# The third depthwise convolution moved from VectorE to ScalarE and GpSimd

## The chip, the cores and the metric

The kernel runs on one core of a Trainium2 chip. The time is the device time of one execution in microseconds; the median of several executions counts. The engines are TensorE (PE in the rows; PEld is its weight load), VectorE (DVE), ScalarE (ACT), GpSimd (POOL) and SyncE (SP).

## The reference

The program is two transformer-like blocks over 512 tokens of 1024 channels in float32. The first block's mixing stage is where the change lies. It projects the normalised input by `w_in` and splits the result. One half is a gated causal depthwise convolution of width 31 over 512 channels, with a layer norm over the channels and a silu:

```
u, u_gate = jnp.split(p_conv, 2, axis=-1)
u = u * jax.nn.sigmoid(u_gate)
u = causal_dwconv(u, conv_dw_w, conv_dw_b)          # 31 taps, 512 channels
u = jax.nn.silu(layer_norm(u, LN_EPS) * conv_ln_g + conv_ln_b)
```

The other half is an RWKV recurrence over 8 heads of 64 (`wkv7_scan`), with its own norm and gate, of which only the cost matters here. Both halves are joined and multiplied by `w_out`. A gated feed-forward follows, and then the second block (attention, feed-forward, HGRN2, feed-forward), which the change does not touch.

## The kernel before, in words

Channels lie on the 128 partitions and the 512 tokens along the free dimension, so the 512 channels of the convolution are four tiles of 128 x 512, here called the first to the fourth convolution (`i` = 0 to 3). Every dense product is made three times with float32 operands split into a high and a low part (lines 193 to 195): weights arrive by a transfer of SyncE's queue, ScalarE makes the high part `wh` (line 168) and VectorE the low part `wl` (line 169).

`conv_in(i)` (line 486) makes the convolution's input `u`: two dense products, a tanh by ScalarE into a tile `s` of the buffer "gate" (line 490), and a product by VectorE (line 491). `conv(i)` (line 493) starts its sum `acc` with a ScalarE operation that takes the first tap and the bias (line 499). The other 30 taps are VectorE operations of line 501, each of which reads the shifted `u` and `acc` and writes `acc`. The trace calls `acc` "h", since it lies in that tensor. `u` has two buffers.

The RWKV half goes by four pairs of heads. For a pair p, `wkv_prep` makes the decays and scores (VectorE masks NM and LM, lines 663 and 664). `wkv_inverse` (line 686) inverts triangular blocks. It begins on GpSimd: a transfer of NM to Ld in DRAM (line 696) and back as small blocks Gb (line 698), 15 products and 15 sums of up to 64 elements on 64 partitions (lines 705 and 707), a transposing copy into Tt (line 709), two transfers to Dd (line 714) and two back as Dm and Dt (line 715). All of these transfers are issued by GpSimd. Then TensorE and ScalarE grow the inverse (lines 717 to 762) in small products, each with a copy out of PSUM by ScalarE (lines 724, 746, 752, 756). `wkv_tail` (line 765) finishes the pair; it takes a tile from each of the single buffers "tl" (`sq`, line 807) and "gate" (`r`, line 812).

`mix_out` (line 889) multiplies by `w_out` in two parts: the first three of eight k-tiles are those of the first three pairs, the other five wait for the convolution's result and the last pair. Between them `conv_tail` (line 539) normalises the four convolutions: mean (line 546), difference (549), squares (551), variance (552), a reciprocal root (566 to 569), silu (558) and the split for the product (252, 253).

The order in each engine's queue is fixed when the program is built. The library that orders it takes an operation when its inputs are ready in a plan of its own and prefers the one that stands earlier in the program; a tile's buffer is given out in the same way. A block under `with filler(k)` (line 143) adds a million to that place, so it goes behind everything else. The third convolution is such a filler (lines 529 and 530), between `wkv_inverse` and `wkv_tail` of the third pair; so are the first part of `w_out` and `conv_tail`. The fourth convolution (line 534) is not.

Of the kernel before, what the change touches and what calls it, by code (L numbers as in the profile page):

```python
# [9 lines left out]
F32 = mybir.dt.float32  # L10
# [4 lines left out]
AF = mybir.ActivationFunctionType  # L15
# [4 lines left out]
P = 128  # L20
D = 1024
KD = 8
T1 = 512
# [53 lines left out]
MULT, ADD, SUB = ALU.mult, ALU.add, ALU.subtract  # L77
# [344 lines left out]
def mix(k):  # L422
    tc, nc, A, vec = k.tc, k.nc, k.A, k.vec
    with ExitStack() as ctx:
        banks(k, ctx, "m", a=3, b=3)
        p1 = ctx.enter_context(tc.tile_pool(name="mx1", bufs=1))
        p2 = ctx.enter_context(tc.tile_pool(name="mx2", bufs=4))
# [65 lines left out]
        def conv(i):  # L493
            acc = S.acc_u[:, i]
            for t in range(CK):
                src = us[i][:, t:t + T1]
                w = S.cw[:, 4 * t + i:4 * t + i + 1]
                if t == 0:
                    nc.scalar.activation(acc, src, AF.Identity, bias=vec("conv_dw_b", i), scale=w)  # L499
                else:  # L500
                    nc.vector.scalar_tensor_tensor(acc, src, w, acc, MULT, ADD)  # L501

# [13 lines left out]
        conv_in(0)  # L516
        gates()
        conv(0)
        wkv_inverse(k, Q[0])
        wkv_tail(k, Q[0])  # L520
        Q[2] = pair(2)
        wkv_inverse(k, Q[1])
        conv_in(1)
        wkv_tail(k, Q[1])
        conv(1)
        Q[3] = pair(3)
        conv_in(2)
        wkv_inverse(k, Q[2])
        with filler(k):
            conv(2)  # L530
# [1049 lines left out]
```

## Time and profile before

| | |
|---|---|
| median of 3 runs (lowest, highest) | 2308.98 us (2307.26, 2311.26) |
| the profiled execution | 2304.93 us |
| its span, first to last instruction | 2303.2 us |
| mean granted TensorE clock, share of full | 0.986 |
| busy share of PE, DVE, ACT, POOL | 97%, 62%, 43%, 4% |
| taps of line 501 on VectorE, all four convolutions | 120 operations, 90.3 us |

The busy shares are means over stages with different limits. The mixing stage with its product by `w_out` is the first 420 us or so of the span. In the rows below, a time at the front of a line is microseconds from the span's start; the second number is how long the operation or the group took; in square brackets stands how long the engine was idle before it and what ended the wait.

### The profile page before, as it was taken

Reading aid. Unit: us, or ns where it says so; the run is one execution under the profiler, and the core shown is the slowest. Engines: PE = TensorE matmul, PEld = TensorE weight load, DVE = VectorE, ACT = ScalarE, POOL = GpSimd, SP = SyncE. Lnnn points to the kernel's source line nnn. Section 1 sums busy time; section 2 is a strip of 40 time slices with the busy share of each in tenths; the row PEclk is TensorE's granted clock in tenths of the full one; section 3 lists DMA queues with packets and bytes.
Section 4 is the critical chain, followed back from the end, with each engine's and each line's share of the span. In section 5 each row is a group of like instructions: output and inputs, shape, how many; then the busy total and the mean of one; then the engine's idle time right before and its main releaser. Section 6 shows DMA issues by size and latency. Waiting matters only on the chain.

```text
span 2303.2 us, 38001 instructions
## 1 busy us (share of the span) xinstructions
PE 2235.7 (97%) x15280; PEld 1990.0 (86%) x15280; DVE 1429.5 (62%) x3022; ACT 979.4 (43%) x1928; POOL 100.7 (4%) x200
## 2 busy tenths in 40 slices
PE   6999798899999999999999999999999999999999
PEld 4677676688888989888899999999999999999888
DVE  6876777875652566666676666335666667666522
ACT  3535344544442465666553444224333335444321
POOL 1150330000000000000000000000000000000000
PEclk8999999899999999999999999999999999999999
DMA  9443221253233532221032222234111113222332
GB/s 318 152 128 122 76 56 55 88 170 101 92 99 95 148 104 81 67 65 53 33 122 92 86 89 92 83 94 117 56 59 62 45 47 114 92 92 92 91 118 76
DMA packets 73936, 220.11 MB, mean 96 GB/s; under 512 B 8976, under 2 KB 17616, under 8 KB 73760
## 3 DMA queue, kind: packets, MB, share of 16 engines
q1 hardware_dynamic: 68064, 206.17, 28.2%
q0 software_dynamic: 2784, 7.82, 1.5%
q10 hardware_dynamic: 2912, 3.69, 0.5%
q8 instruction: 121, 1.98, 0.4%
q14 instruction: 55, 0.45, 0.1%
HBM read 211.24 MB, written 6.85 MB: 95 GB/s over the span
## 4 chain that ended last, share of the span: by engine, by line
PE 88%; DVE 6%; ACT 3%; DMA 1%; issue 1%; SPq 0%; ACTq 0%; DVEq 0%
PE mm L194 24%; PE mm L193 24%; PE mm L195 23%; PE sb L1402 3%; DVE wl L169 1%; PE sc L1217 1%; PE sb L1192 1%; PE sa L660 1%; ACT wh L168 1%; PE sc L1235 1%; PE sa L865 1%; PE sa L1122 1%; DMA ada<-ada_wT 1%; DMA Dm<-Dd 0%; PE sb L745 0%
## 5 line engine op out<-in xcount | busy, mean ns | idle before, releaser
L193 PE MATMUL mm<-xh,wh 128*128 128x264 f32 (+4 forms) x2852 | 904.8, 317 | 11.0 <-ACT xh L252 5.7
L194 PE MATMUL mm<-xh,wl 128*128 128x264 f32 (+4 forms) x2852 | 895.8, 314 | 4.8 <-DVE wl L169 4.5
L195 PE MATMUL mm<-xl,wh 128*128 128x264 f32 (+4 forms) x2852 | 892.5, 313 | 0.1
L193 PEld LDWEIGHTS mm<-xh,wh 128*128 128x128 f32 x2852 | 536.2, 188 | 46.6 <-ACT xh L252 6.7
L194 PEld LDWEIGHTS mm<-xh,wl 128*128 128x128 f32 x2852 | 536.4, 188 | 39.3 <-DVE wl L169 8.4
L169 DVE TENSOR_TENSOR wl<-ws,wh 128x1024 fp32r<-128x1024 f32 (+3 forms) x358 | 399.9, 1117 | 273.6 <-ACT wh L168 272.8
L195 PEld LDWEIGHTS mm<-xl,wh 128*128 128x128 f32 x2852 | 536.9, 188 | 30.5 <-issue 2.1
L168 ACT CAST wh<-ws 128x1024 fp32r<-128x1024 f32 (+3 forms) x358 | 344.8, 963 | 479.1 <-PE mm L195 410.2
L194 PE MATMUL mm<-gh,wl 128*128 128x264 f32 (+2 forms) x792 | 253.3, 320 | 1.3 <-DVE wl L169 0.9
L193 PE MATMUL mm<-gh,wh 128*128 128x264 f32 (+2 forms) x792 | 252.9, 319 | 0.0
L195 PE MATMUL mm<-gl,wh 128*128 128x264 f32 (+2 forms) x792 | 252.7, 319 | 0.0
L194 PEld LDWEIGHTS mm<-gh,wl 128*128 128x128 f32 x792 | 149.6, 189 | 13.2 <-DVE wl L169 2.8
L193 PEld LDWEIGHTS mm<-gh,wh 128*128 128x128 f32 x792 | 149.5, 189 | 10.5
L195 PEld LDWEIGHTS mm<-gl,wh 128*128 128x128 f32 x792 | 149.6, 189 | 10.2
L975 DVE SCALAR_TENSOR_TENSOR fz<-mm,V,fz 128x511 f32<-128x511 f32 x88 | 65.9, 749 | 63.2 <-ACT fz L973 61.7
L501 DVE SCALAR_TENSOR_TENSOR h<-u,cw,h 128x512 f32<-128x512 f32 x120 | 90.3, 752 | 1.8 <-ACT h L499 0.5
L1402 PE MATMUL sb<-q,kt 128*128 128x64 f32 (+3 forms) x592 | 75.7, 272 | 2.2 <-DVE kt L1434 2.2
L1402 PEld LDWEIGHTS sb<-q,kt 128*128 128x128 f32 x592 | 73.5, 195 | 2.8 <-DVE kt L1434 1.0
L194 PE MATMUL mm<-oh,wl 128*128 128x264 f32 x256 | 74.9, 292 | 0.6 <-DVE wl L169 0.6
L193 PE MATMUL mm<-oh,wh 128*128 128x264 f32 x256 | 74.8, 292 | 0.1
L195 PE MATMUL mm<-ol,wh 128*128 128x264 f32 x256 | 74.4, 291 | 0.0
L973 ACT ACTIVATE fz<-mm,V 128x512 f32<-128x512 f32 x44 | 34.2, 777 | 59.9 <-PE mm L195 59.9
(512 smaller groups left out, 2828.6 us busy)
## 6 DMA issues: line engine op xcount, KB each, us to landing
ws<-w_up_t SPq DMA_DIRECT2D x44, 512.0 KB, 3.5
ws<-gate_t SPq DMA_DIRECT2D x44, 512.0 KB, 3.5
ws<-up_t SPq DMA_DIRECT2D x44, 512.0 KB, 3.5
ws<-down_t SPq DMA_DIRECT2D x34, 512.0 KB, 3.5
wa<-ada_wT SPq DMA_DIRECT2D x32, 512.0 KB, 3.7
ws<-fox_in_t SPq DMA_DIRECT2D x32, 512.0 KB, 3.5
ws<-hg_in_t SPq DMA_DIRECT2D x32, 512.0 KB, 3.5
ws<-w_in_t SPq DMA_DIRECT2D x22, 512.0 KB, 3.8
```

The lines of the kernel that those rows point to most:

```text
L168: nc.scalar.copy(hi[:, :n], st[:, :n])
L169: nc.vector.tensor_sub(lo[:, :n], st[:, :n], hi[:, :n])
L193: mm(o, hi[:, w], xh[i][:, a:b], start=start and i == 0, stop=False)
L194: mm(o, lo[:, w], xh[i][:, a:b], start=False, stop=False)
L195: mm(o, hi[:, w], xl[i][:, a:b], start=False, stop=stop and i == n - 1)
L501: nc.vector.scalar_tensor_tensor(acc, src, w, acc, MULT, ADD)
L660: nc.tensor.matmul(sc[hh][:, kind], lt[r, cs], ar[r, c], start=True, stop=True)
L865: nc.tensor.matmul(sq.ps[:, :n], k.mean, t, start=i == 0, stop=i == KD - 1)
L973: nc.scalar.activation(z, ps, AF.Identity, bias=vec("ffn_dw_b", nt), scale=wt(2))
L975: nc.vector.scalar_tensor_tensor(z[:, t:], ps[:, 0:T1 - t], wt(2 - t), z[:, t:], MULT, ADD)
L1122: nc.tensor.matmul(s, k.blk, sq[:, hs(j)], start=True, stop=True)
L1402: nc.tensor.matmul(o, kt[:, a:a + P], qv, start=True, stop=True)
```

## The change

For the third convolution (`i == 2`) a tap after the first is no longer one operation of VectorE. ScalarE multiplies the shifted input by the tap's weight into a new tile `m`, and GpSimd adds `m` to `acc`. `m` takes the existing single buffers "gate" and "tl" by turns. The first tap, the other three convolutions and the place in the program stay as they are.

```diff
                 if t == 0:
                     nc.scalar.activation(acc, src, AF.Identity, bias=vec("conv_dw_b", i), scale=w)
+                elif i == 2:
+
+                    m = p2.tile([P, T1], F32, name="cvm", tag=("gate", "tl")[t % 2], bufs=1)
+                    nc.scalar.activation(m, src, AF.Copy, scale=w)
+                    nc.gpsimd.tensor_tensor(acc, acc, m, op=ADD)
                 else:
                     nc.vector.scalar_tensor_tensor(acc, src, w, acc, MULT, ADD)
```

## Rows read from the trace of the kernel before

**Rows 1.** The page: busy time and instructions of each engine; GpSimd's busy tenths.

```profile
PE 2235.7 (97%) x15280; PEld 1990.0 (86%) x15280; DVE 1429.5 (62%) x3022; ACT 979.4 (43%) x1928; POOL 100.7 (4%) x200
...
POOL 1150330000000000000000000000000000000000
```

**Rows 2.** Busy time by stretch: start:end, length, busy us of each engine (instructions).

```profile
290.00:301.50 11.50, 11.50 (x94) 8.60 (x95) 9.71 (x21) 4.58 (x16) 0.00 (x0) 1.00 0.06 17
301.50:333.50 32.00, 30.15 (x241) 21.70 (x235) 25.64 (x42) 11.91 (x32) 17.85 (x37) 1.00 0.27 65
333.50:378.50 45.00, 44.99 (x334) 33.05 (x334) 35.56 (x59) 20.25 (x44) 0.10 (x1) 1.00 0.19 58
378.50:395.00 16.50, 8.75 (x23) 4.80 (x22) 10.41 (x17) 11.59 (x18) 0.00 (x0) 0.90 0.18 52
```

**Rows 3.** The timeline of TensorE around its two gaps.

```profile
331.26 0.39 PE L195 MATMUL mm<-xl,wh 128*128 128x512 f32 x1
333.51 1.16 PE L723 MATMUL sb<-Dm,NM 128*128 128x128 f32 x8 [1.86 <-DMA Dm<-Dd]
...
378.47 0.39 PE L195 MATMUL mm<-xl,wh 128*128 128x512 f32 x1
...
390.58 0.79 PE L193 MATMUL mm<-xh,wh 128*128 128x512 f32 x1 [5.68 <-ACT xh L252]
```

**Rows 4.** The timeline of VectorE: first and last taps of the third and fourth convolution.

```profile
293.78 1.53 DVE L501 SCALAR_TENSOR_TENSOR h<-u,cw,h 128x512 f32<-128x512 f32 x2
...
332.72 0.75 DVE L501 SCALAR_TENSOR_TENSOR h<-u,cw,h 128x512 f32<-128x512 f32 x1
...
339.66 1.54 DVE L501 SCALAR_TENSOR_TENSOR h<-u,cw,h 128x512 f32<-128x512 f32 x2 [0.47 <-ACT h L499]
...
374.74 0.75 DVE L501 SCALAR_TENSOR_TENSOR h<-u,cw,h 128x512 f32<-128x512 f32 x1
```

**Rows 5.** Line 501 by itself: duration in ns as least/median/most, first and last start.

```profile
L501 DVE SCALAR_TENSOR_TENSOR h<-u,cw,h x120: 721/747/1100, 114.5 to 374.7; 128x512 f32<-128x512 f32 x120
```

**Rows 6.** The timeline of GpSimd: the fourth pair's inverse.

```profile
301.54 0.94 POOL L696 DMA_DIRECT2D Ld<-NM  x1 [24.29 <-DVE NM L663]
307.04 0.84 POOL L698 DMA_DIRECT2D Gb<-Ld  x1 [4.56 <-DMA Ld<-NM]
310.14 0.21 POOL L705 TENSOR_TENSOR tm<-Gb,Tb 64x15 f32<-64x15 f32 x1 [2.26 <-DMA Gb<-Ld]
...
316.22 0.31 POOL L707 TENSOR_TENSOR Tb<-Tb,tm 64x64 f32<-64x64 f32 x1
...
324.48 0.62 POOL L709 COPY Tt<-Tb 64x256 f32<-64x256 f32 x1
...
328.59 0.91 POOL L715 DMA_DIRECT2D Dm<-Dd  x1 [1.84 <-ACT sq L813]
329.49 0.89 POOL L715 DMA_DIRECT2D Dt<-Dd  x1
```

**Rows 7.** Line 606 by itself, a ScalarE operation with a scale, SBUF to SBUF.

```profile
L606 ACT ACTIVATE sq<-kx,V x4: 709/712/716, 65.6 to 253.8; 128x512 f32<-128x512 f32 x4
```

**Rows 8.** The timeline of all engines: a GpSimd copy and a tap beside it.

```profile
249.73 0.60 POOL L709 COPY Tt<-Tb 64x256 f32<-64x256 f32 x1
249.89 1.00 DVE L501 SCALAR_TENSOR_TENSOR h<-u,cw,h 128x512 f32<-128x512 f32 x1
```

**Rows 9.** The timeline of all engines: VectorE beside small GpSimd operations, first and last.

```profile
245.19 0.79 DVE L816 SCALAR_TENSOR_TENSOR y<-y,lg,r 128x512 f32<-128x512 f32 x1
...
246.18 0.61 POOL L707 TENSOR_TENSOR Tb<-Tb,tm 64x48 f32<-64x48 f32 x1
...
248.53 0.78 DVE L501 SCALAR_TENSOR_TENSOR h<-u,cw,h 128x512 f32<-128x512 f32 x1
```

**Rows 10.** The timeline of ScalarE: a weight cast and the fourth gate's tanh.

```profile
322.24 0.51 ACT L168 CAST wh<-ws 128x384 fp32r<-128x384 f32 x1 [7.55 <-PE mm L195]
...
336.61 0.60 ACT L490 ACTIVATE gate<-mm 128x512 f32<-128x512 f32 x1
```

## The prediction

> **What bounds the kernel now.** I read the page first: the span is 2303.2 us, TensorE is busy in 97% of it, and GpSimd only in the first seven of the 40 slices, which is the mixing stage [rows 1]. Then the busy time of each engine in four stretches around the third convolution [rows 2]. From 290 to 378.5 us TensorE has almost no gap (86.64 of 88.5 us), VectorE is busy for 70.9 us, ScalarE for 36.7 and GpSimd for 18. From 378.5 to 395 TensorE is busy for only 8.75 of 16.5 us. So two places could give time back or lose it: the gap of 1.86 us before the matmul at 333.51, which waits for the transfer into Dm, and the long hole from 378.9 to 390.6, in which TensorE waits for the convolutions' normalisation (its mean and variance products are the only work in it) [rows 3].
>
> Where the convolutions stand in VectorE's queue decides the second. The third convolution (the one that changes) runs its 30 taps from 293.78 to 333.5 us, while TensorE has other work. The fourth runs from 339.66 to 375.5, at 45 us almost the whole of the third stretch, and its last tap is at once followed by the normalisation that TensorE then waits for [rows 4]. So the third convolution is off the path as it stands; the fourth one's end is on it. Any time that the edit costs VectorE after 339.66 moves the hole, and so the end, by as much.
>
> **Part one, what leaves VectorE.** 30 operations of 0.747 us (the median of line 501, [rows 5]) are 22.4 us, all before 333.5. TensorE idles for 1.86 us there, so this can return 1.9 us at most, and only by way of GpSimd, whose inverse of the fourth pair ends in the transfer that the gap waits for. That chain (from the Ld transfer at 301.54 to the Dm transfer at 328.59, [rows 6]) holds 30 small products and sums from 310.14 to 324.48: 14.3 us. With their undisturbed durations of 0.21 to 0.31 us and 0.08 between two, they would take about 10.3 us; the 4 us more are spent beside VectorE's operations. I take half of it as the taps' part: 2 us earlier.
>
> **Part two, ScalarE.** 30 products, each like the Square with a scale of 128x512 from SBUF to SBUF of line 606, 0.712 us [rows 7]: 21.4 us. ScalarE has 51.8 us free from 290 to 378.5 [rows 2], so as a load they cost nothing. As a wait they can cost: a small copy out of PSUM that stands behind a product is late by up to 0.71 us, and the product itself waits for its buffer (only two: "gate" and "tl", which `wkv_tail` and `conv_in` use too). I count 0 here and leave the rest to a rival.
>
> **Part three, GpSimd.** No addition of 128x512 is in the trace. Nearest are those of 64 partitions: 15 elements in 0.21 us, 64 in 0.31 [rows 6]. That is 2.04 ns an element, so 512 make 0.31 + 448 x 2.04 ns = 1.22 us, 1.30 from start to start with the 0.08 gap. From below the bound is the copy of 256 elements, 0.60 [rows 8]; from above, four times the copy (twice the elements, two inputs instead of one), 2.4. I take 1.30: 30 of them are 39 us in a chain, since each adds to the same tile.
> They can begin at 291.3 (the bias tap of line 499, then a product). Until the Ld transfer at 301.54 GpSimd does nothing: 8 additions. Its waits for transfers (302.48 to 307.04, 307.88 to 310.14, 326.75 to 328.59) take 3, 1 and 1 more. 17 are left after the Dt transfer is issued at 330.4, so they run from there to 352.5 alone, or to about 365 if each waits for an operation of VectorE (0.75). Placed in those waits, an addition is in the way of the next link at up to four points (Ld, Gb, first product, Dm) for half its 1.30 on average, 2.6 us in all. Against the 2 us of part one that leaves the Dm transfer, and with it the fourth convolution's start, 0.6 later; from 2 earlier (of which the gap holds 1.9) to 5.2 later.
>
> **Part four, what GpSimd takes from VectorE.** At 249.73 GpSimd copies 256 elements; the tap that VectorE starts at 249.89 takes 1.00 us instead of 0.747: 0.25 us lost [rows 8]. With the small operations nothing is lost: the five operations of VectorE from 245.19 to 248.53 start 0.668 apart beside GpSimd's sums of 39 to 48 elements, which themselves stretch to 0.6 [rows 9]. So the two engines exclude each other, and a long operation of GpSimd holds VectorE's. An addition reads 2 x 512 elements, four times the copy's 256: 4 x 0.25 = 1.0 us for each addition that meets a VectorE operation of two SBUF inputs (the taps, the weight splits of line 169). Bounds: 0, as for the small sums, and 1.30, the whole addition. I take 1.0, which the slope (512 x 2.04 ns) gives as well.
> The Trainium skill, SBUF — State Buffer, section "SBUF: two separate sides", says that VectorE and GpSimd share one pair of ports as an exclusive lock, held for the whole instruction, and that the other blocks fully. By the whole of 1.30 us the sum below would be 5 us larger; rows 9 speak against the whole instruction, since the small sums hold VectorE for next to nothing.
> The 13 additions before 330.4 fall where VectorE has just lost 22.4 us of work; they cost nothing. The 17 later ones fall on the fourth convolution: 17 x 1.0 = 17 us of holding, in a stretch of 45 us in which VectorE has 9.4 us to spare [rows 2]. If all of that absorbs, 7.6 us are lost; if none, 17. These gaps are waits for other engines in the order of the queue, so I let two thirds (6.3) absorb: 10.7 us.
>
> **The sum.** 0.6 + 10.7 = 11.3 us, all through the end of the fourth convolution. The profiled execution took 2304.93 us (span 2303.2 and 1.7 around it), so 2316.2 in its terms; the median of the runs lies 4.05 us above that execution, so 2320.
>
> **The rivals.**
> *A, queues block (slower still).* The orders of the queues are fixed beforehand. If additions beside VectorE run slower than the order allows for (1.30 alone, 2.0 with a tap between), the product for the next addition but one stands at the head of ScalarE's queue until its buffer is free, and behind it stand the PSUM copies of the fourth inverse, which TensorE uses at once. For: TensorE has no gap from 333.5 to 378.5 that could absorb it. Against: ScalarE is idle for more than half. 17 x 0.7 = 12 us of waiting beside the 10.7; partly the same time, so about 20 us: 2329. The buffers add to it: `wkv_tail` holds "tl" and "gate" again from 367.7, so a third convolution not done by then ends after 376.
> *B, hidden.* VectorE holds GpSimd rather than the other way round, or most of the additions come before 330. Then only the 0.6 remain: about 2309, no change. For: rows 9, where GpSimd gave way at no cost. Against: row 249.89, and 39 us of additions do not fit before 330.4.
> *C, faster.* The product behind the fourth convolution's gate is done by 322.2 (the weight cast that its buffer releases starts at 322.24), yet its tanh runs at 336.61 [rows 10], behind other ScalarE work and after "gate" came free. The second product ends at 331.65 [rows 3]. If the new order, with VectorE free and "gate" given out otherwise, puts that tanh before 331, the fourth convolution starts 6 us earlier and the normalisation with it. It wins from the point where the additions hold VectorE for less than those 6 us after 333 plus the spare: with half the holding (8.5, of which 6.3 is absorbed) it is -6.2 + 2.2 = -4 and the gap's 1.9: 2303. Against: "gate" is wanted by 15 products more.
> The Trainium skill, GPSIMD Engine Reference, section "4.1 Engine selection", advises VectorE for elementwise additions and calls GpSimd about twice as slow with two inputs; my 1.22 against 0.747 us is a ratio of 1.6, and a ratio of 2 would make the 17 additions 5 us longer. No run here shows it yet.
>
> **Chances.** Forecast 0.45 (2314 to 2328), A 0.20 (2325 to 2345), B 0.20 (2305 to 2313), C 0.15 (2298 to 2304). A measurement of this kernel can tell about 0.2% (4.6 us) from no change, so slower is 0.65, the same 0.20, faster 0.15. Likeliest: 2320. The range leaves out most of C and the upper end of A: 2305 to 2336.
>
> **What would show it.** Right: the fourth convolution's taps spread past 380, single taps of 1.3 to 2 us after 333, additions of 1.2 to 2 us on GpSimd until 350 to 365, and the hole before TensorE's matmul of 390.58 about 11 us later, with nothing after it changed. Part three is wrong if the additions take under 1 us or over 2.4 alone; part four if the taps keep 0.75 beside them. The whole is wrong if the third convolution's additions are done before 335, or if the fourth convolution starts before 334.

## The result, and the profile after

The changed kernel takes 2327.48 us (median of 4 runs, 2325.29 to 2332.21) against 2309.49 us before (4 runs, 2307.26 to 2311.26): a ratio of 1.0087, with a 95% interval of 1.0064 to 1.011. That is 18.0 us slower. The profiled execution took 2325.29 us against 2304.93, so 20.4 us more in the traces (spans 2323.5 and 2303.2).

All of it arises in the mixing stage. The hole before the matmul of line 193 ends at 411.58 us instead of 390.58 [rows 3], 21.0 later; from there to the end the two traces need 1911.9 and 1912.6 us. The busy time by stretch, which answers to [rows 2], with the columns as there:

```profile
290.00:301.50 11.50, 10.07 (x89) 7.30 (x87) 4.74 (x13) 10.05 (x26) 8.82 (x7) 1.00 0.06 18
301.50:333.50 32.00, 25.61 (x207) 19.50 (x207) 3.88 (x11) 18.29 (x39) 29.85 (x50) 0.87 0.11 28
333.50:378.50 45.00, 40.42 (x298) 28.80 (x299) 25.59 (x41) 20.90 (x43) 13.74 (x12) 0.91 0.20 52
378.50:395.00 16.50, 13.53 (x51) 8.68 (x48) 15.58 (x25) 7.84 (x13) 0.10 (x1) 0.95 0.17 45
```

VectorE, relieved of 30 taps, has almost nothing to do from 301.5 to 333.5 us (3.88 us busy, before 25.64). GpSimd is full in its place (29.85), and TensorE, which had gaps of 1.9 us in the second stretch and none in the third, now has 6.4 and 4.6 us of them. The new operations themselves, one line each (ns as least/median/most), and the two waits between them in this stage:

```profile
L504 POOL TENSOR_TENSOR h<-h,cvm x30: 1252/1272/1700, 291.8 to 346.1; 128x512 f32<-128x512 f32 x30
L503 ACT ACTIVATE cvm<-u,cw x30: 708/722/727, 291.0 to 344.7; 128x512 f32<-128x512 f32 x30
...
ACT cvm L503 <- POOL h L504: 20.6, 17, 3.4
POOL h L504 <- ACT cvm L503: 15.5, 2, 15.1
```

Of the last two lines the second is harmless: GpSimd had been idle before its first addition anyway. The first is not. 17 products stand at the head of ScalarE's queue until an addition frees their buffer, 20.6 us in all.

GpSimd's timeline, which answers to [rows 6], shows where the additions went (a line with x3 is three in a row):

```profile
291.82 8.02 POOL L504 TENSOR_TENSOR h<-h,cvm 128x512 f32<-128x512 f32 x6 [15.07 <-ACT cvm L503]
300.30 3.99 POOL L504 TENSOR_TENSOR h<-h,cvm 128x512 f32<-128x512 f32 x3 [0.46 <-ACT cvm L503]
304.23 0.95 POOL L701 DMA_DIRECT2D Ld<-NM  x1
...
309.99 4.00 POOL L504 TENSOR_TENSOR h<-h,cvm 128x512 f32<-128x512 f32 x3
313.94 0.21 POOL L710 TENSOR_TENSOR tm<-Gb,Tb 64x15 f32<-64x15 f32 x1
...
315.72 1.26 POOL L504 TENSOR_TENSOR h<-h,cvm 128x512 f32<-128x512 f32 x1
316.95 0.26 POOL L710 TENSOR_TENSOR tm<-Gb,Tb 64x48 f32<-64x48 f32 x1
...
333.09 1.26 POOL L504 TENSOR_TENSOR h<-h,cvm 128x512 f32<-128x512 f32 x1
334.30 0.95 POOL L714 COPY Tt<-Tb 64x256 f32<-64x256 f32 x1
...
336.89 3.41 POOL L504 TENSOR_TENSOR h<-h,cvm 128x512 f32<-128x512 f32 x2
340.25 0.92 POOL L720 DMA_DIRECT2D Dm<-Dd  x1
...
342.07 5.50 POOL L504 TENSOR_TENSOR h<-h,cvm 128x512 f32<-128x512 f32 x4
```

Nine additions precede the Ld transfer, three and three stand in the waits for Ld and Gb, and then nine stand between the small operations of the inverse, which are links of one chain: each behind a sum, eight of them ahead of the next product and one ahead of the copy. Two more wait ahead of the Dm transfer and four come after it. The Ld transfer is 2.7 us later than before, the first small product 3.8, the copy into Tt 9.8, the Dm transfer 11.7.

ScalarE's timeline, around what answers to [rows 10]:

```profile
332.70 0.72 ACT L503 ACTIVATE cvm<-u,cw 128x512 f32<-128x512 f32 x1 [1.00 <-POOL h L504]
333.33 0.49 ACT L168 CAST wh<-ws 128x384 fp32r<-128x384 f32 x1
...
344.71 0.72 ACT L503 ACTIVATE cvm<-u,cw 128x512 f32<-128x512 f32 x1 [0.62 <-POOL h L504]
...
346.06 0.63 ACT L812 ACTIVATE sq<-y 128x512 f32<-128x512 f32 x1 [0.23 <-POOL h L504]
...
350.20 0.69 ACT L817 ACTIVATE r<-sa,mat 128x512 f32<-128x512 f32 x1
...
355.61 0.60 ACT L490 ACTIVATE gate<-mm 128x512 f32<-128x512 f32 x1
```

The weight cast that ran at 322.24 [rows 10] now runs at 333.33, behind products that wait. VectorE's timeline shows who waits for it, and the fourth convolution, which answers to [rows 4]:

```profile
333.86 0.92 DVE L169 TENSOR_TENSOR wl<-ws,wh 128x384 fp32r<-128x384 f32 x1 [7.78 <-ACT wh L168]
334.69 0.67 DVE L806 TENSOR_TENSOR y<-y,sa 128x512 f32<-128x512 f32 x1
335.65 1.80 DVE L253 TENSOR_TENSOR xl<-h,xh 128x512 fp32r<-128x512 f32 x1 [0.28 <-ACT xh L252]
...
359.35 4.69 DVE L506 SCALAR_TENSOR_TENSOR h<-u,cw,h 128x512 f32<-128x512 f32 x6 [0.96 <-ACT h L499]
...
395.16 0.75 DVE L506 SCALAR_TENSOR_TENSOR h<-u,cw,h 128x512 f32<-128x512 f32 x1
```

Behind that split stands `y`, a step of the third pair's tail; after it the tail's square `sq`, which follows the last products. The same steps in the kernel before, `y` on VectorE, the square and the root `r` on ScalarE:

```profile
321.56 0.69 DVE L801 TENSOR_TENSOR y<-y,sa 128x512 f32<-128x512 f32 x1
...
324.99 0.63 ACT L807 ACTIVATE sq<-y 128x512 f32<-128x512 f32 x1 [0.96 <-DVE y L805]
...
326.93 0.69 ACT L812 ACTIVATE r<-sa,mat 128x512 f32<-128x512 f32 x1
```

So `y` is 13.1 us later and the square 21.1. In the kernel before `y` stood ahead of its split (326.84) in VectorE's queue, so the edit changed the order of the queue as well as the waits. The fourth convolution starts 19.7 us later than at 339.66 [rows 4], and then its taps run at their usual 0.75 us: the last addition ended at 347.6.

So the 19.0 us by which the fourth gate's tanh is late (355.61 against 336.61) have two parts. TensorE's first matmul with Dm comes at 345.09, 11.6 us later than in [rows 3]; that is GpSimd's queue. Before, the tail's root `r` was done (326.93) while that transfer was awaited, and the tanh followed the matmul by 3.1 us. Now the square and the root come after the matmul, and the tanh follows it by 10.5: 7.4 us more, which is ScalarE's queue. About 1 us of these is TensorE's: between the square and the root it runs the product of line 815 in 2.08 us instead of 1.12 (line 810 before), at a granted clock of 0.50 from 346 to 348, after it had waited for Dm. Both traces need about the same from the fourth convolution's first tap to the end of the hole (50.9 and 52.2 us).

### The profile page after: what moved, and what is told of

Its sections match the earlier page's. It is cut to its first block, busy times and chain, and to the rows that moved or that the text cites. A ratio compares the mean times of both kernels' runs of the same rounds, so it can differ in the third digit from the quotient of the medians.

```text
span 2323.5 us, 38051 instructions
## 1 busy us (share of the span) xinstructions
PE 2243.0 (97%) x15280; PEld 1994.7 (86%) x15280; DVE 1409.7 (61%) x2992; ACT 1000.3 (43%) x1958; POOL 137.1 (6%) x230
## 4 chain that ended last, share of the span: by engine, by line
PE 86%; DVE 6%; ACT 3%; POOL 2%; issue 1%; DMA 1%; SPq 0%; ACTq 0%; DVEq 0%; POOLq 0%
PE mm L194 23%; PE mm L193 23%; PE mm L195 23%; PE sb L1407 3%; POOL h L504 1%; DVE wl L169 1%; PE sc L1222 1%; PE sb L1197 1%; PE sc L1240 1%; ACT wh L168 1%; PE sa L665 1%; PE sa L1127 1%; PE sa L870 1%; DVE h L506 1%; DMA ada<-ada_wT 1%
## 5 line engine op out<-in xcount | busy, mean ns | idle before, releaser
L194 PEld LDWEIGHTS mm<-xh,wl 128*128 128x128 f32 x2852 | 537.9, 189 | 41.9 <-DVE wl L169 10.3
L506 DVE SCALAR_TENSOR_TENSOR h<-u,cw,h 128x512 f32<-128x512 f32 x90 | 67.2, 747 | 1.6 <-ACT h L499 1.0
```

The source lines that it names most:

```text
L194: mm(o, lo[:, w], xh[i][:, a:b], start=False, stop=False)
```

## The experiments

Theory 1 is GpSimd's queue: the additions between the links of the inverse make the Dm transfer late. Theory 2 is ScalarE's queue with the two buffers: a product waits at its head, and the tail and the fourth gate behind it. The prediction's own theory is that the additions hold VectorE's taps. Diffs are against the changed kernel unless the kernel before is named; the ratios are to the kernel before, run on the same chip.

**Additions without products** (the weights of the 30 taps are left out).

```diff
-                    m = p2.tile([P, T1], F32, name="cvm", tag=("gate", "tl")[t % 2], bufs=1)
-                    nc.scalar.activation(m, src, AF.Copy, scale=w)
-                    nc.gpsimd.tensor_tensor(acc, acc, m, op=ADD)
+                    nc.gpsimd.tensor_tensor(acc, acc, src, op=ADD)
```

> GpSimd adds the shifted input itself to the sum (the weights of 30 taps of the third convolution are left out), so the 30 additions stay on GpSimd, but ScalarE has no products and the buffers gate and tl are not touched. Theory 1 (GpSimd's queue: additions between the links of the fourth pair's inverse make its transfer into Dm late, and all that follows with it): still slower by 8 us or more, 2317 to 2328, the Dm transfer issued at 336 or later instead of 328.6. Theory 2 (ScalarE's queue and the two shared buffers: products that wait for a buffer hold up the third pair's tail, whose buffer the fourth convolution's gate needs): the loss is gone, 2305 to 2313, the Dm transfer at most 4 us late and the fourth convolution starting before 344. The prediction's own theory (additions hold VectorE's taps): taps of the fourth convolution of 1.3 us and more.

2326.78 us, 1.0067 [1.0048, 1.0087]. Without a product to wait for, 17 additions go ahead of the Ld transfer. GpSimd's timeline, then TensorE's:

```profile
311.65 0.94 POOL L699 DMA_DIRECT2D Ld<-NM  x1
...
345.32 0.91 POOL L718 DMA_DIRECT2D Dm<-Dd  x1 [1.85 <-DMA Dd<-Tb]
```

```profile
350.22 2.08 PE L726 MATMUL sb<-Dm,NM 128*128 128x128 f32 x8 [15.26 <-DMA Dm<-Dd]
```

The tail and the tanh are not late here (square at 327.39, tanh at 333.51), yet the fourth convolution begins at 353.34, behind the copies of the late inverse. GpSimd's queue alone is enough for most of the loss; the interval reaches that of the changed kernel.

**Products in a pair of their own**, so that no buffer is shared with the tail or the gate.

```diff
+            if i == 2:
+                ms = p2.tile([P, 2, T1], F32, name="cvm", tag="wa", bufs=1)
...
-                    m = p2.tile([P, T1], F32, name="cvm", tag=("gate", "tl")[t % 2], bufs=1)
+                    m = ms[:, t % 2]
```

> The changed kernel, but the products go to two halves of a buffer of their own (the one of the modulation weights, idle by then) instead of gate and tl. ScalarE still makes 30 products with two places, GpSimd 30 additions. Theory 1: as slow as the changed kernel, 2323 to 2330, the fourth convolution's first tap after 352. Theory 2 in its buffer half (the tail of the third pair waits for tl): that tail's square runs as soon as its input is there instead of at 346, first tap of the fourth convolution before 348, 2312 to 2320. Theory 2 in its queue half (products at the head of ScalarE's queue): no better than the changed kernel.

2327.51 us, 1.0071 [1.0047, 1.0095]: no better. In ScalarE's timeline the products wait as before (17.1 us in all), since the pair is as deep as the two buffers were, and the square comes straight behind one. The trace is of the slowest of the five executions (2334.5 us), so its places are later than those of the changed kernel:

```profile
350.44 0.72 ACT L505 ACTIVATE cvm<-u,cw 128x512 f32<-128x512 f32 x1 [0.97 <-POOL h L506]
351.07 0.61 ACT L814 ACTIVATE sq<-y 128x512 f32<-128x512 f32 x1
```

With the additions on GpSimd, sharing "gate" and "tl" is not what costs.

**Additions on VectorE**, products as in the change.

```diff
-                    nc.gpsimd.tensor_tensor(acc, acc, m, op=ADD)
+                    nc.vector.tensor_add(acc, acc, m)
```

> The changed kernel with the additions on VectorE instead of GpSimd: the products of ScalarE and the buffers gate and tl stay. Theory 1: the loss is gone, 2306 to 2313. Theory 2: the products wait for VectorE's additions (about 0.7 us) instead of GpSimd's 1.27, so about half the loss stays: 2314 to 2320, ScalarE still waiting for buffers with over 8 us in all.

2320.41 us, 1.0045 [1.0029, 1.0062]: half of the loss without an addition on GpSimd. The Dm transfer is early (326.67), which theory 1 wanted, but the tanh comes at 348.02. ScalarE's timeline:

```profile
333.71 0.59 ACT L729 COPY ys<-sb 128x512 f32<-128x512 f32 x1 [7.41 <-PE sb L728]
334.19 1.33 ACT L503 ACTIVATE cvm<-u,cw 128x512 f32<-128x512 f32 x2
335.67 0.72 ACT L503 ACTIVATE cvm<-u,cw 128x512 f32<-128x512 f32 x1 [0.15 <-DVE h L504]
336.47 0.63 ACT L812 ACTIVATE sq<-y 128x512 f32<-128x512 f32 x1
...
348.02 0.60 ACT L490 ACTIVATE gate<-mm 128x512 f32<-128x512 f32 x1
```

The last products stand behind a copy that waits 7.41 us for TensorE, and the square, whose input was ready at 321.5, stands behind them. VectorE waits 13.5 us for products in this stage. The time is at the edge of what theory 2 expected, but not by the wait that it named: ScalarE waits only 4.5 us for buffers, not over 8.

**The same with the pair of their own** (both edits above).

> The additions on VectorE, as in the run before that had them there, and the products in two halves of a tile of their own instead of in gate and tl. There the third pair's tail had its y ready at 321.5 us, but its square, which takes tl, came at 336.5, after the last product and its addition. If the shared buffers put it there, the square comes at 322 to 326 now, the fourth gate's tanh before 338, and the loss of 0.45% goes: 2306 to 2312 us. If the products at the head of ScalarE's queue put it there, which their own buffers don't change (as they did not with the additions on GpSimd), the square stays at 334 or later and the time at 2315 to 2321.

2320.15 us, 1.0052 [1.004, 1.0064]. Each expectation is half right. The square does come as soon as its input is there (329.74, `y` at 329.01, in an execution whose Ld transfer is already some 5 us late), so in the run before it was the shared buffer that held it back. But the time stays. VectorE's timeline shows what replaces it, a step of the tail behind an addition that waits for a product:

```profile
343.62 0.69 DVE L506 TENSOR_TENSOR h<-h,cvm 128x512 f32<-128x512 f32 x1 [4.90 <-ACT cvm L505]
344.23 0.75 DVE L824 SCALAR_TENSOR_TENSOR y<-y,V,vx 128x512 f32<-128x512 f32 x1
```

A buffer of its own moves the wait from one queue to the other; what costs, as these two traces read, is that each tap now needs two queues in step.

**Products that nobody adds** (the change without its last line; 30 taps are left out).

```diff
-                    nc.gpsimd.tensor_tensor(acc, acc, m, op=ADD)
```

> ScalarE makes the 30 products into gate and tl, nobody adds them (30 taps of the third convolution are left out). Each product's buffer is free as soon as it is written. If the load of 21.4 us on ScalarE costs the time that products with VectorE's additions cost (about 10 us over the kernel before), this one costs it too: 2318 to 2323. If it is the wait of a product at the head of ScalarE's queue for the addition before it, the loss is gone: 2305 to 2313, with no wait of ScalarE for a buffer over 0.5 us and the fourth convolution's first tap before 344.

2305.17 us, 0.9988 [0.9975, 1.0]. The 30 products run from 293.7 to 324.0 at a median of 0.712 us and never wait for a buffer; the tanh is at 335.09. ScalarE's 21 us cost nothing as a load, and the 22 us that VectorE is spared buy nothing, or the two cancel within the 0.25% that the interval leaves. Only as a wait do the products cost.

**The additions beside the fourth convolution alone.** Kernel before, with 17 additions that nothing uses, put behind the fourth inverse.

```diff
         wkv_inverse(k, Q[3])
+        with filler(k):
+            ms = p2.tile([P, T1], F32, name="cvm", tag="wa", bufs=1)
+            for t in range(17):
+                nc.gpsimd.tensor_tensor(ms, us[3][:, t:t + T1], us[3][:, t + 1:t + 1 + T1], op=ADD)
         conv(3)
```

> The kernel before with 17 more GpSimd additions of 128x512, whose sums nobody uses, put behind the fourth pair's inverse in GpSimd's queue, so that they run beside the fourth convolution's taps and stand in front of nothing. This is the price that the prediction put on them: if each holds VectorE for 1.0 us and 6.3 us are absorbed, the fourth convolution ends 11 us later and the time is 2317 to 2323, with taps of 1.5 us and more. If GpSimd gives way, or VectorE's spare time takes it all, 2308 to 2313.

2311.9 us, 1.0019 [1.0006, 1.0032], less than the prediction's theory expects. GpSimd's timeline, with the additions by themselves (ns as least/median/most), and VectorE's:

```profile
334.71 23.24 POOL L537 TENSOR_TENSOR cvm<-u 128x512 f32<-128x512 f32 x17 [7.62 <-DVE u L491]
...
L537 POOL TENSOR_TENSOR cvm<-u x17: 1033/1367/1370, 334.7 to 356.6; 128x512 f32<-128x512 f32 x17
```

```profile
337.93 2.37 DVE L501 SCALAR_TENSOR_TENSOR h<-u,cw,h 128x512 f32<-128x512 f32 x2 [0.52 <-ACT h L499]
...
340.89 5.20 DVE L501 SCALAR_TENSOR_TENSOR h<-u,cw,h 128x512 f32<-128x512 f32 x4
346.01 1.39 DVE L169 TENSOR_TENSOR wl<-ws,wh 128x384 fp32r<-128x384 f32 x1
347.33 4.41 DVE L501 SCALAR_TENSOR_TENSOR h<-u,cw,h 128x512 f32<-128x512 f32 x3
...
354.09 4.41 DVE L501 SCALAR_TENSOR_TENSOR h<-u,cw,h 128x512 f32<-128x512 f32 x3
```

So the holding is real: in rows beside additions a tap takes 1.30 to 1.47 us (each row's time by its taps) instead of 0.78 in a row alone. Against rows alone, the twelve taps lose 7.1 us, the two splits of line 169 and one of line 253 another 1.6: 8.7 us, 0.5 for each addition. How much of the 8.7 reaches the end, this trace cannot tell. The convolution takes 41.8 us in it (337.93 to 379.72) instead of 35.8 [rows 4], but TensorE's granted clock is 0.50 from 346 to 358 here and 1.00 in the kernel before; and with no addition beside it the fourth convolution takes 40.6 us in the run of products that nobody adds (clock 0.50 from 350 to 358). The medians put it at 0.19%, some 4 us of the 8.7.

**Eight additions.** The pair of its own, and the product and addition only for `t <= 8`; the other 22 taps return to VectorE.

```diff
-                elif i == 2:
+                elif i == 2 and t <= 8:
```

> The changed kernel with only taps 1 to 8 as products and additions (in two places of a buffer of their own), the other 22 on VectorE. All eight additions stand in front of the Ld transfer in GpSimd's queue, none between the links of the fourth pair's inverse or behind them. If the loss comes from additions between those links and products that wait for them, it is gone: 2306 to 2314, Ld issued at most 2 us late and the fourth convolution's first tap within 3 us of 339.7. If any product and addition pair costs (about 20 us for 30), 8 of them cost about 5: 2314 to 2318.

2313.51 us, 1.0019 [1.0005, 1.0033]. All eight come before the Ld transfer, none between links; products wait 0.9 us in all. Most of the loss of the change is gone. The time is in the first range, near its upper end, and both of the places named for it were missed: the Ld transfer comes at 307.35, 5.8 us late, and the fourth convolution's first tap at 343.78, 4.1 late. The additions are not what Ld waits for there: GpSimd is done with them and idle for 1.5 us until VectorE's mask NM comes.

**The gate's buffer in the kernel before.** Its tanh tile `s` for the fourth convolution in the idle buffer "wa".

```diff
-            s = p2.tile([P, T1], F32, name="gate", bufs=1)
+            s = p2.tile([P, T1], F32, name="gate", tag="wa" if i == 3 else "gate", bufs=1)
```

> The kernel before with one edit: the tanh of the fourth convolution's gate goes to a buffer of its own (the one of the modulation weights) instead of gate, so it need not wait for the third pair's tail. All taps on VectorE. If the start of the fourth convolution sets the end of the stage, its first tap comes at about 333.5 instead of 339.7 and the time falls by as much of these 6 us as the third convolution's last taps don't take back: 2303 to 2306. If the start doesn't matter (TensorE's other work ends at 378.9 anyway and the normalisation waits for something else): 2309, no change.

2306.96 us, 0.9978 [0.9962, 0.9994]: the fastest version, and faster than both kernels. The tanh runs at 319.27 instead of 336.61, as soon as its product is there. The fourth convolution's start gains only 5.6 us of those 17, in ScalarE's timeline:

```profile
319.27 0.60 ACT L490 ACTIVATE gate<-mm 128x512 f32<-128x512 f32 x1 [7.56 <-PE mm L195]
...
333.18 0.81 ACT L499 ACTIVATE h<-u,V,cw 128x512 f32<-128x512 f32 x1
```

Its end gains less still: the last tap ends at 374.80 instead of 375.49. The convolution takes 40.8 us instead of 35.8, because steps of the fourth pair stand between its taps in VectorE's queue, and these are not earlier by as much (TensorE's first matmul with Dm at 331.50 instead of 333.51). An early start alone does not make an early end.

**Both, eight additions and that buffer.**

> The eight taps of the run before, and the fourth gate's tanh in a buffer of its own, which made the kernel before faster by 0.2%. If the eight taps cost nothing and free VectorE before the fourth convolution starts, the gain of the buffer stays or grows by up to 2 us: 2302 to 2307. If they cost a few us, they eat it: 2308 to 2314.

2308.97 us, 1.0001 [0.9989, 1.0013]. The buffer's gain and the additions' loss cancel, as the second expectation has it. Even eight additions that stay off the inverse's links buy nothing.

## Why the prediction was right in its number and wrong in its steps

The time lies in the range, the sign is right, and 2327.48 is 7.5 us above the 2320 forecast. But the 11.3 us of the sum were made of 0.6 for a late start of the fourth convolution and 10.7 for taps held back there, and the trace shows 19.7 for the start and nothing for the taps, so that the number came out is luck. The step that failed is the one in part three: "that leaves the Dm transfer, and with it the fourth convolution's start, 0.6 later; from 2 earlier [...] to 5.2 later". The transfer was 11.7 later, outside its bounds. The second is the wait of the products that part two put at 0: with TensorE's slower product it made the fourth gate's tanh another 7.4 later.

*Part one*, no gain from VectorE's 22.4 us, is right: no end moved earlier. That the small operations of the inverse run faster without the taps is right too, and by more than I took. From the first product to the Tt copy the chain took 14.34 us before [rows 6] and 20.36 after; the nine additions in it hold the next link up by 11.0 us (1.21 to 1.24 each, start to start), so the small operations alone took 9.4. That is 5.0 gained, not 2. In the run of products that nobody adds, with neither taps nor additions beside it, the chain took 10.39 (312.53 to 322.92): the estimate of 10.3 was good, and the whole difference of 4 was the taps' part, not half of it. The rest of the 5.0 is mostly the nine gaps of 0.08 that the additions fill.

*Part two* is right as a load (0.722 us against 0.712 [rows 7], and the products that nobody adds cost nothing) and wrong in leaving the wait at 0. I had named both things behind a product, the small copies and the two buffers, and given the whole to a rival. The fourth convolution was misread as well: it takes 35.8 us (339.66 to 375.49) of the stretch of 45, not 45, and between its last tap and the normalisation lie 3 us of other VectorE operations.

*Part three* has the right price: 1.272 us in the median against 1.22 estimated, and nine additions before Ld against eight. The Trainium skill, GPSIMD Engine Reference, section "4.1 Engine selection", calls GpSimd about twice as slow with two inputs; the same addition took 0.692 us where it ran on VectorE, so 1.84 times, which agrees. What it missed is the place. I let additions fill GpSimd's waits for transfers and put the other 17 behind the inverse. But the order that was built lets additions in between links too, behind nine of the sums (why there, the trace does not show). So nine went between links, at 1.2 us each where a 0.08 us gap had been. The working is: 3.8 late at the first product, plus 11.0, less 5.0, is the 9.8 at Tt; the copy (0.95 us, before 0.62) and the two additions ahead of the Dm transfer (1.70 and 1.63) make it 11.7.

*Part four* did not happen in the changed kernel, because with most additions done among the links none was left at 359. Only splits were held there: the three of 333.86, 335.65 and 338.14 took 3.7 us together instead of 1.9. Where I made it happen to taps, an addition held VectorE for 0.5 us, not 1.0: the slope from one copy [rows 8] was twice too steep. The share that reaches the end (guessed as 10.7 of 17, 63%) is about half by the medians (some 4 of 8.7, with an interval from 1.4 to 7.4 us). The Trainium skill, SBUF — State Buffer, section "SBUF: two separate sides", has the lock held for the whole instruction. Beside each other, additions of 1.37 us back to back and single taps of 1.41 make one tap per addition, 1.45 us a pair from start to start; one after the other, with the addition's 1.03 alone and the tap's 0.75, it would be 1.8. So the trace agrees that the two exclude each other in part, and not for the whole instruction.

*Rival A* comes nearest, in time (2329) and kind: products at the head of ScalarE's queue, behind them what TensorE uses. It placed them at the fourth inverse's copies after 333, with 10.7 from the taps beside it. They waited 20.6 us from 294 on, and what stood behind them was a weight cast and the third pair's tail. *B* had its condition, since 22 of the 30 additions begin before 330 and not the 13 of part three, and fell all the same: early additions are not hidden where they stand in the inverse's chain. *C*'s mechanism is real in the kernel before, where a buffer for the fourth gate gives 0.22%, 5 us of the 6 that it hoped for; in the changed kernel the tanh moved the other way.

The two halves do not seem to add. GpSimd's queue alone costs 0.67%, products with additions on VectorE 0.45 and 0.52%, both together 0.87% in the changed kernel and 0.71% with the pair. Their intervals reach 0.12 to 0.24% to either side, so it is not shown that both together cost more than GpSimd's queue alone. The traces read as if the fourth convolution waits for the later of the two and for the work between them.

What stays open is where the 0.19% of the eight additions come from. In both traces that have them TensorE idles 1.4 us in the 4 us before 302 and before 298, behind ScalarE's copies that now stand after products, and a spell at 0.50 as in the last section follows; the kernel before has neither. But the changed kernel has the same idle time in the 4 us before 298.5 and no spell until 318, so the cause is not shown. Open too is how much the new order of the queues costs and how much the waits in it: no run keeps the order and changes the waits alone.

## What to carry to other kernels

Before an operation goes to an idle engine, look at what the idle time between that engine's operations is: a gap in a chain of short dependent operations is not room, and work of low priority that gets in there delays every later link. Splitting one operation into two on different engines ties two in-order queues together, and the price is what stands behind the half that waits, whether or not either engine is busy. A forecast whose total is right can have its terms wrong, so check the place of each term in the trace, not the sum.

## What the runs showed that was not expected

The granted clock falls in this stage in some executions and not in others. In the kernel before it is 1.00 in every 4 us from 286 to 390. In the run with eight additions TensorE is at the lower level (1.2 GHz, 0.50) twice, though it is busy throughout; stretches of its trace, columns as in [rows 2]:

```profile
302.00:306.00 4.00, 4.00 (x14) 2.79 (x14) 0.23 (x1) 2.32 (x7) 3.28 (x3) 0.50 0.00 0
306.00:310.00 4.00, 4.00 (x35) 2.91 (x33) 2.71 (x6) 1.42 (x5) 0.94 (x1) 0.50 0.30 86
...
358.00:362.00 4.00, 4.00 (x21) 2.06 (x19) 0.57 (x2) 1.83 (x4) 0.00 (x0) 0.50 0.00 0
362.00:366.00 4.00, 4.00 (x21) 3.55 (x21) 2.91 (x4) 0.87 (x3) 0.00 (x0) 0.50 0.18 49
```

Each pair of lines is 8 us at half speed, so 4 us of work lost. In that run TensorE had been idle for 1.4 of the 4 us before 302. In the run of additions without products the clock fell to 0.50 from 310 to 318 with no gap since 286. In the changed kernel it is 0.51 and 0.63 in the 8 us from 318 to 326, after 1.6 us of idle time; there TensorE then waits for `y` until 335.42, so that spell did not set the end. Such spells are worth as much as the effects compared here: the hole ends 10.6 us later in that profile than in [rows 3], while the medians differ by 0.19% (4.4 us). Places are read from single traces here, amounts from the medians. Behind the longest waits the clock is low as well, so a wait costs a second time: after TensorE's 6.98 us (additions on VectorE) and 15.26 us (additions without products) of waiting for Dm, the eight matmuls that follow take 2.08 us at a granted clock of 0.50, against 1.16 us at 1.00 after 1.86 us of waiting in [rows 3].

The second thing is that both engines pay where they meet. With VectorE idle the first addition of the run with 17 of them took 1.03 us, and beside taps they take 1.37; a single tap goes from 0.75 to 1.41. In the changed kernel the additions at 336.89 and 338.67 took 1.70 and 1.63 us instead of 1.27, beside splits of 1.80 and 1.00 instead of 0.69.
